# Seven block products for eight in groups 6 to 10 of the first feed-forward part, with that part's order written out, and block 2's first three groups moved to its end

## The chip, the cores and the metric

The kernel runs on one core of a Trainium2 chip. The metric is the device time of one execution in microseconds (us). A core has a matrix engine (PE, with its weight loads as PEld), a vector engine (DVE), an activation engine (ACT), a general engine (POOL) and an engine that issues most DMAs (SP). Each works through its own list of instructions in order and waits for the others by semaphores.

## The reference

One layer of a streaming encoder in fp32: 1024 prompt frames and 32 sample frames, model width 1024, feed-forward width 2816.

```python
x += 0.5 * gate1 * RMSNorm(SwiGLU_1(adaLN(RMSNorm(x))))    # first feed-forward part (FFN1)
x +=       gate2 * RMSNorm(W_out [mixerA ; mixerB](adaLN(RMSNorm(x))))
x += 0.5 * gate3 * RMSNorm(SwiGLU_2(adaLN(RMSNorm(x))))    # second feed-forward part (FFN2)
def swiglu(h, w_gate, w_up, w_down):
    return (jax.nn.silu(h @ w_gate) * (h @ w_up)) @ w_down
# shift, scale and gate of all three: SiLU(c) @ w_mod + b_mod   (1024 -> 9216)
```

Mixer A is a chunked attention of 8 heads, mixer B a sliding-window attention of 8 query and 2 key/value heads; one projection w_in (1024 -> 2304) feeds both. New key and value rows are outputs too.

## The kernel before

**Number format.** Every fp32 operand is split into a rounded part (hi, by ACT) and the rest (lo, by DVE), and a product is three matmuls: hi·hi, hi·lo, lo·hi (`mm3`, L339 to L341). So each weight tile that is loaded costs an ACT copy and a DVE subtraction before PE can use it, the "split".

**Tiling.** The 1056 frames are three token blocks: 0 and 1 of 384 columns, 2 of 288 (256 prompt and 32 sample). The 22 tiles of 128 feed-forward columns are 11 groups of two. For a group and a block the kernel forms gate and up (96 matmuls of the block's width), silu times up (`sl`, `gg`, DVE L904 and L907, ACT L903), and the down product (`dn`, 48 matmuls), which DVE adds into the block's accumulator `facc`.

**FFN1** (`ffn_plain`) goes through groups 0 to 7 with all blocks, then groups 8 to 10 with blocks 0 and 1, and last groups 8 to 10 with block 2, whose weights are loaded again. While block 2's groups run, block 0 and then block 1 get their residual, norm and next input (`between`: `resid` writes `f` by L485 and L488, `norm_h` writes `n` by L441 and `h` by L467, with a chain of small operations L348 to L352 for one over the root). The loads of w_in for the mixers are issued there too. Beside FFN1, generators that `step` moves on by one piece work out w_mod's product on DVE (`mod_aside`, L241 and L243), since no matmul is used for it.

**FFN2** (`ffn`) does groups 0 and 1 block by block, and groups 2 to 10 with all blocks as "fast" rounds. In those gate and up of blocks 0 and 1 are one product of two by two blocks (feed-forward tile, half of the model width, token block), made by seven block products instead of eight in a scheme of Strassen's kind: `STRASSEN` lists them, L595 issues their matmuls, `Mat` forms sums of weight blocks, `combos` the sums T1 to T4 of inputs. Block 2 has no partner and is done as usual with the same weight tiles (`g`, L595). The order of DVE, ACT and PE in the fast rounds is the order in which the code is written (`manual_schedule`); elsewhere a scheduler orders each engine's list when the kernel is built. In both, the list of an engine is fixed on the chip. The order of a round's stages is gate of the round, down of the one before, up of the round.

Of the kernel before, what the change touches and what calls it, by code (L numbers as in the profile page):

```python
# [78 lines left out]
def encoder_step(ctx: ExitStack, tc, x_prompt, x_sample, cache_a_k, cache_a_v, cache_b_k, cache_b_v,  # L79
# [109 lines left out]
    def mod_chunk(n):  # L189
        raws = []  # L190
        for g in range(2):
            r = t_tile("w", [128, 4, 512], "wm")
# [17 lines left out]
        coefs(n)  # L210

    def coefs(n):

        seg, half = divmod(n, 2)
        c0 = 8 * seg + 4 * half
        cs, ks = slice(c0, c0 + 4), slice(4 * half, 4 * half + 4)
        ve.tensor_tensor(modT[:, :, cs], modT[:, :, cs],
                         cst[:, None, cs].to_broadcast([128, 2, 4]), op=OP.add)
        sub, kind = divmod(seg, 3)
        if kind == 1:  # L220
            ve.scalar_tensor_tensor(acoef[:, sub, :, ks], modT[:, :, cs], 1.0,
                                    gain(2 * sub)[:, None, ks].to_broadcast([128, 2, 4]),
                                    op0=OP.add, op1=OP.mult)
        elif kind == 2:
            ve.scalar_tensor_tensor(gcoef[:, sub, :, ks], modT[:, :, cs], 1.0 if sub == 1 else 0.5,
                                    gain(2 * sub + 1)[:, None, ks].to_broadcast([128, 2, 4]),
                                    op0=OP.mult, op1=OP.mult)
# [1484 lines left out]
```

## Time and profile before

| | |
|---|---|
| median of 3 runs | 2184.54 us (2183.96 to 2186.63) |
| the profiled execution, its span | 2184.44 us, 2182.7 us |
| PE busy | 2123.9 us (97%) |
| DVE, ACT, POOL busy | 1403.6 (64%), 786.3, 171.8 us |
| TensorE clock granted, mean | 0.985 |

FFN1 takes the span from about 45 to 850 us, the mixers to about 1415, FFN2 the rest. Busy time is a share of an average over stages; a window of the trace tells which engine is full in one stage. A wait names the instruction that ended it.

### The profile page before, as it was taken

What the parts mean: (1) busy time and instruction counts of PE and PEld (TensorE: products, weight loads), DVE (VectorE), ACT (ScalarE), POOL (GpSimd) and SP (SyncE); (2) the same over time, 40 slices, a digit from 0 to 9 for tenths busy, and PEclk for the clock granted to TensorE, in tenths of its full rate; (3) what the DMA queues carried; (4) which work ended last, traced back from release to release, by engine and by line L of the source; (5) the groups of instructions that cost most, each with busy time, mean ns of one, the idle gap of its engine ahead of it and who ended that gap; (6) DMA issues with size and microseconds to landing.
All of it is one profiled execution on the core that took longest, in us unless ns stands there. A gap on an engine that the chain in (4) does not pass through costs nothing.

```text
span 2182.7 us, 34270 instructions
## 1 busy us (share of the span) xinstructions
PE 2123.9 (97%) x13796; PEld 2029.4 (93%) x13796; DVE 1403.6 (64%) x2783; ACT 786.3 (36%) x1654; POOL 171.8 (8%) x273
## 2 busy tenths in 40 slices
PE   6999999999999999899999899999999999999998
PEld 4999999999999999898888578999999999999997
DVE  5687667865343497677544776589666656566658
ACT  3411111111121254467544665365432222233225
POOL 1100000000000022100100323220000000000001
PEclk8999999999999999899999899999999999999999
DMA  9253334433121244100210202244311111111114
GB/s 319 103 155 116 107 97 135 136 91 115 55 78 58 87 152 141 60 25 26 69 31 26 84 22 86 98 160 129 113 62 55 39 59 39 58 59 39 39 59 140
DMA packets 178803, 192.35 MB, mean 88 GB/s; under 512 B 7788, under 2 KB 147476, under 8 KB 177492
## 3 DMA queue, kind: packets, MB, share of 16 engines
q1 hardware_dynamic: 178644, 190.16, 28.1%
q8 instruction: 108, 1.77, 0.3%
q14 instruction: 51, 0.42, 0.1%
HBM read 170.42 MB, written 22.86 MB: 89 GB/s over the span
## 4 chain that ended last, share of the span: by engine, by line
PE 88%; DVE 6%; DMA 3%; ACT 2%; issue 1%; POOL 0%; SPq 0%; DVEq 0%; ACTq 0%; POOLq 0%
PE g L595 5%; PE dn L339 4%; PE gate L341 4%; PE gate L340 4%; PE dn L340 4%; PE dn L341 4%; PE up L339 4%; PE up L341 4%; PE gate L339 4%; PE up L340 4%; PE ga L595 3%; PE gb L595 3%; PE gd L595 3%; PE dn L807 3%; PE dn L805 3%; PE dn L806 3%
## 5 line engine op out<-in xcount | busy, mean ns | idle before, releaser
L318 DVE TENSOR_TENSOR w<-raw,w 128x1024 fp32r<-128x1024 f32 x109 | 135.0, 1243 | 80.7 <-ACT w L317 80.6
L805 PE MATMUL dn<-gg,w 128*128 128x384 f32 (+1 forms) x528 | 170.1, 323 | 1.7 <-DVE facc L812 1.7
L339 PE MATMUL dn<-gg,w 128*128 128x384 f32 (+1 forms) x528 | 170.0, 324 | 1.0 <-DVE facc L934 0.9
L541 ACT ACTIVATE w<-raw 128x512 fp32r<-128x512 f32 x180 | 110.1, 626 | 169.0 <-issue 75.8
L806 PE MATMUL dn<-gg,w 128*128 128x384 f32 (+1 forms) x528 | 169.1, 321 | 1.8 <-DVE gg L700 1.8
L382 POOL TENSOR_TENSOR sq<-sq 128x384 f32<-128x384 f32 (+1 forms) x48 | 53.0, 1114 | 1491.2 <-ACT sq L378 1460.4
L340 PE MATMUL dn<-gg,w 128*128 128x384 f32 (+1 forms) x528 | 169.7, 321 | 0.6 <-DVE gg L907 0.6
L807 PE MATMUL dn<-gg,w 128*128 128x384 f32 (+1 forms) x528 | 168.9, 322 | 1.2 <-DVE w L542 1.2
L341 PE MATMUL dn<-gg,w 128*128 128x384 f32 (+1 forms) x528 | 169.4, 321 | 0.0
L317 ACT ACTIVATE w<-raw 128x1024 fp32r<-128x1024 f32 x109 | 114.4, 1056 | 145.1 <-PE up L341 48.8
L812 DVE TENSOR_TENSOR facc<-dn,facc 128x768 f32<-128x768 f32 (+1 forms) x120 | 106.5, 890 | 89.7 <-PE dn L807 89.7
L934 DVE TENSOR_TENSOR facc<-dn,facc 128x768 f32<-128x768 f32 (+1 forms) x120 | 106.0, 887 | 81.3 <-PE dn L341 81.3
L243 DVE SCALAR_TENSOR_TENSOR macc<-raw,csil,macc 128x512 f32<-128x512 f32 x196 | 137.7, 747 | 15.2 <-DMA raw<-in_w_mod_dram 14.8
L542 DVE TENSOR_TENSOR w<-raw,w 128x512 fp32r<-128x512 f32 x180 | 124.8, 705 | 19.5 <-ACT w L541 19.1
L903 ACT ACTIVATE sl<-gate 128x384 f32<-128x384 f32 (+1 forms) x66 | 30.5, 463 | 283.1 <-PE gate L341 280.3
L595 PE MATMUL g<-h_hi,w 128*128 128x288 f32 x576 | 123.2, 294 | 0.0
L340 PE MATMUL gate<-h,w 128*128 128x384 f32 x352 | 118.6, 337 | 1.9 <-DVE h L467 1.9
L339 PE MATMUL gate<-h,w 128*128 128x384 f32 x352 | 118.7, 337 | 0.0
L341 PE MATMUL gate<-h,w 128*128 128x384 f32 x352 | 118.3, 336 | 0.0
L339 PE MATMUL up<-h,w 128*128 128x384 f32 x352 | 118.1, 335 | 0.0
L341 PE MATMUL up<-h,w 128*128 128x384 f32 x352 | 118.1, 335 | 0.0
L340 PE MATMUL up<-h,w 128*128 128x384 f32 x352 | 117.9, 335 | 0.0
(318 smaller groups left out, 5787.5 us busy)
## 6 DMA issues: line engine op xcount, KB each, us to landing
raw<-in_w_gate_dram SPq DMA_DIRECT2D x58, 512.0 KB, 3.9
raw<-in_w_up_dram SPq DMA_DIRECT2D x58, 512.0 KB, 4.1
raw<-in_w_down_dram SPq DMA_DIRECT2D x58, 512.0 KB, 3.6
raw<-in_w_mod_dram SPq DMA_DIRECT2D x56, 512.0 KB, 3.9
raw<-in_w_in_dram SPq DMA_DIRECT2D x18, 512.0 KB, 4.4
wm<-in_w_mod_dram SPq DMA_DIRECT2D x8, 1024.0 KB, 7.1
raw<-in_w_out_dram SPq DMA_DIRECT2D x13, 512.0 KB, 4.6
xr<-xs SPq DMA_DIRECT2D x16, 384.0 KB, 3.5
```

The source lines that it names most:

```text
L243: ve.scalar_tensor_tensor(acc[j], r[:, kk], c, acc[j], op0=OP.mult, op1=OP.add)
L317: ae.activation(w[:, 0], r, AF.Copy)
L318: ve.tensor_sub(w[:, 1], r, w[:, 0])
L339: te.matmul(ps, w[:, 0, k], hi, start=start, stop=False)
L340: te.matmul(ps, w[:, 0, k], lo, start=False, stop=False)
L341: te.matmul(ps, w[:, 1, k], hi, start=False, stop=stop)
L541: ae.activation(w[:, 0], src, AF.Copy)
L542: deferred.append(lambda: ve.tensor_tensor(w[:, 1], src, w[:, 0], op=OP.subtract))
L595: te.matmul(ps, w[a][:, k, :], x[b][k], start=first and k == 0 and q == 0, stop=last and k == n - 1 and q == 2, skip_group_check=True)
L805: te.matmul(ps[:, s, :w], h[:, k % 4, :], g[:, 0, :w], start=q == 0, stop=False)
L806: te.matmul(ps[:, s, :w], h[:, k % 4, :], g[:, 1, :w], start=False, stop=False)
L807: te.matmul(ps[:, s, :w], l[:, k % 4, :], g[:, 0, :w], start=False, stop=q == 1)
```

## The change

FFN1 now uses `ffn` as well, under the key "h1". Its rounds are groups 0 to 2 with blocks 0 and 1, groups 3 to 10 with all three, and groups 0 to 2 with block 2 at the end (weights loaded again). Groups 6 to 10 are fast rounds. From the gate of group 3 to the gate of the first of block 2's rounds at the end, the order of DVE, ACT and PE is the written one; ahead of that and behind it the scheduler orders as before. The first round does gate and then up of a block, and up's weights lie in tiles `wu`. w_mod's product is made in pieces of 384 columns instead of 512, the first quarter of it by ACT; its last eight of 72 column tiles are worked out in FFN2. The hi and lo parts of inputs T1 to T3 are formed ahead of the first fast round and T4 in it. FFN1 has pools of its own (`FFN1`), and the mixers' pools are opened (`open_pools("mx")`) only behind it, ahead of the first loads of w_in. Splits are of 512 columns everywhere in FFN1 (before: 1024).

```diff
-STEPS = 6
+LAST = 3
+PLAIN = 6
+FFN1 = {"ux": 3, "r": 4, "w": 4, "g": 6, "s": 11}
...
-    open_pools("mx", **MIX)
+    open_pools("f1", **FFN1)
...
-    def rounds():
+    def rounds(key):
         both, n = (0, 1, 2), NF // 2
-        return [(g, (tb,)) for tb in both for g in range(LEAD)] + [(g, both) for g in range(LEAD, n)]
+        if key == "h3":
+            return [(g, (tb,)) for tb in both for g in range(LEAD)] + [(g, both) for g in range(LEAD, n)]
+        return [(g, (0, 1)) for g in range(LAST)] + [(g, both) for g in range(LAST, n)] + \
+            [(g, (2,)) for g in range(LAST)]
...
-        fast = {r for r, (g, t) in enumerate(plan) if len(t) == 3}
+        fast = {r for r, (g, t) in enumerate(plan) if len(t) == 3 and (key == "h3" or g >= PLAIN)}
+        fixed = (min(fast), len(plan) - 1) if key == "h3" else (LAST, NF // 2)
...
-            if (r, what) == (len(plan) - 1, "u"):
+            if (r, what) == (fixed[1], "u" if key == "h3" else "g"):
+                flush()
                 steady.close()
...
+            elif key == "h1" and r == 0:
+                mu = loaded[r, "u"]
+                mu.places = wide() + [t_tile("r", [128, 2, 4, 128], "w", F32R)]
+                for tb in blocks:
+                    need((key, tb))
+                    last = tb == blocks[-1]
+                    plain(r, "g", m, [tb], lambda k: None)
+                    plain(r, "u", mu, [tb], lambda k, last=last: last and ready(i + 2, k))
...
-    ffn1 = ffn_plain("h1", H1, F1, w1_gate, w1_up, w1_down, mod_rest, "h2", lambda tb: between(F1[tb], tb, 0, H2))
+    ffn1 = ffn("h1", H1, (("T3", "ux"), ("T1", "u"), ("T2", "ux"), ("T4", "u")), F1, lambda tb: u_tile(tb, "facc", F32),
+               w1_gate, w1_up, w1_down, "h2", lambda tb: between(F1[tb], tb, 0, H2, p1 if tb == 1 else pc), mod_rest)
...
+    open_pools("mx", **MIX)
     wkv, wq0, wv0 = split_vcols(w_in, 2048), load_qb(0), load_va(0)
```

Three places show how the lists move. The first is DVE at FFN1's start, where block 1's first norm is made (`rt`, `ry`: the small chain; `n`, `h`: block 1's input; `w`, `wu`: splits of weights). Before, from the last steps of the chain:

```order
L351 SCALAR_TENSOR_TENSOR rt<-rt,rv 128x3
L352 SCALAR_TENSOR_TENSOR ry<-rt,ry 128x3
L907 TENSOR_TENSOR gg<-sl,gg 128x384
L441 SCALAR_TENSOR_TENSOR n<-xt,acoef,pr 128x384 x8
L467 SCALAR_TENSOR_TENSOR h<-n,modT,h 128x384 x3
L932 COPY facc<-dn 128x768 x2
L467 SCALAR_TENSOR_TENSOR h<-n,modT,h 128x384 x3
```

And in the change:

```order
L384 SCALAR_TENSOR_TENSOR rt<-rt,rv 128x3
L385 SCALAR_TENSOR_TENSOR ry<-rt,ry 128x3
L475 SCALAR_TENSOR_TENSOR n<-xt,acoef,pr 128x384 x8
L501 SCALAR_TENSOR_TENSOR h<-n,modT,h 128x384
L576 TENSOR_TENSOR wu<-raw,wu 128x512 x3
L501 SCALAR_TENSOR_TENSOR h<-n,modT,h 128x384 x5
```

The lo parts of up's first three weight tiles now stand behind block 1's eight `n`. PE's list at the same place, in the change (`pss`, `pr`: sum and broadcast of block 1's norm):

```order
L404 MATMUL pss<-ones,sq 128x1 x6
L452 MATMUL pr<-ident,ry 128x128 x3
L632 MATMUL up<-h,wu 128x384 x4
L632 MATMUL gate<-h,w 128x384 x4
L632 MATMUL up<-h,wu 128x384 x32
L632 MATMUL up<-h,w 128x384 x12
L632 MATMUL gate<-h,w 128x384 x20
```

Block 1's `pr` stands behind 48 gate matmuls of block 0; before, it stood behind block 0's gate, up and the first of its down matmuls.

The second place is DVE at FFN1's end, in the second of block 2's three rounds (`dn` of 576 columns is block 2's). The change, from behind the add of the last down product of the first of those rounds to the lo parts of `gg` of the second, in two pieces that follow each other:

```order
L384 SCALAR_TENSOR_TENSOR rt<-rt,rv 128x3
L385 SCALAR_TENSOR_TENSOR ry<-rt,ry 128x3
L576 TENSOR_TENSOR wd<-raw,wd 128x512
L385 SCALAR_TENSOR_TENSOR ry<-rt,ry 128x3
L576 TENSOR_TENSOR wd<-raw,wd 128x512
L475 SCALAR_TENSOR_TENSOR n<-facc,acoef,pr 128x384 x8
L576 TENSOR_TENSOR wd<-raw,wd 128x512
L519 SCALAR_TENSOR_TENSOR facc<-facc,gcoef,pr 128x384 x6
L501 SCALAR_TENSOR_TENSOR h<-n,modT,h 128x384 x3
L519 SCALAR_TENSOR_TENSOR facc<-facc,gcoef,pr 128x384 x2
L501 SCALAR_TENSOR_TENSOR h<-n,modT,h 128x384 x2
L753 TENSOR_TENSOR sl<-sl,up 128x288
```

```order
L576 TENSOR_TENSOR w<-raw,w 128x512
L501 SCALAR_TENSOR_TENSOR h<-n,modT,h 128x384
L522 TENSOR_TENSOR facc<-facc,xr 128x768
L576 TENSOR_TENSOR w<-raw,w 128x512
L753 TENSOR_TENSOR sl<-sl,up 128x288
L576 TENSOR_TENSOR w<-raw,w 128x512 x2
L278 TENSOR_REDUCE modT<-pmt 128x3
L576 TENSOR_TENSOR wd<-raw,wd 128x512
L755 TENSOR_TENSOR gg<-sl,gg 128x288
L522 TENSOR_TENSOR facc<-facc,xr 128x768
L415 TENSOR_TENSOR sq<-sq 128x384
L755 TENSOR_TENSOR gg<-sl,gg 128x288
```

Before, block 0's `n` and `h` stood with block 2's adds, and block 1's residual (`facc<-facc,gcoef,pr`) in a later stretch:

```order
L934 TENSOR_TENSOR facc<-dn,facc 128x576 x2
L441 SCALAR_TENSOR_TENSOR n<-facc,acoef,pr 128x384 x8
L467 SCALAR_TENSOR_TENSOR h<-n,modT,h 128x384 x3
L934 TENSOR_TENSOR facc<-dn,facc 128x576
L467 SCALAR_TENSOR_TENSOR h<-n,modT,h 128x384 x2
L934 TENSOR_TENSOR facc<-dn,facc 128x576
```

So in the change the norm of block 0 and the residual of block 1 stand in one stretch ahead of one round's `gg`.

The third place is SP's list where FFN1 ends and the mixers' first loads stand. Before:

```order
L315 DMA raw<-in_w_down_dram 128x1024 x2
L482 DMA xr<-xs_123 128x768
L331 DMA raw<-in_w_in_dram 128x4x256
L482 DMA xr<-xs_123 128x768
L331 DMA raw<-in_w_in_dram 128x4x256
L482 DMA xr<-xs_123 128x768 x2
L315 DMA raw<-in_w_in_dram 128x8x128
```

The change:

```order
L618 DMA raw<-in_w_down_dram 128x1024 x2
L562 DMA xs_126<-facc 128x3072
L1401 DMA cbk<-in_cache_b_k_dram 128x128
L1402 DMA cbv<-in_cache_b_v_dram 128x128
L338 DMA bias_s<-skew_B 32x160 x8
L364 DMA raw<-in_w_in_dram 128x4x256 x2
L348 DMA raw<-in_w_in_dram 128x8x128
```

w_in's first loads moved behind block 1's write-back (`xs_126`), behind the caches and eight small bias loads; `cbk` waits for the last `gg` of FFN1 there, since the mixers' pools now take over FFN1's space.

More of the change, by code (lines that the diff above doesn't have):

```diff
@@ L209, in mod_chunk @@
                          axis=AX.X, op=OP.add)
[L210 to L227, printed above, removed]
@@ new lines, in encoder_step, with mod_all, fetch @@
+    depth = [2]
+    def mod_all(first, last):
+        pieces = [(c0, g) for c0 in range(first, last, 3) for g in range(4)]
+        tiles = {}
+        def fetch(i):
+            if i < len(pieces):
+                c0, g = pieces[i]
+                w = 128 * min(3, last - c0)
+                r = tiles[i] = h_tile([128, 2, 384], "wma")[:, :, :w]
+                dma.dma_start(r, w_mod[0, 256 * g:256 * (g + 1), 128 * c0:128 * c0 + w]
+                              .rearrange("(k p) n -> p k n", p=128))
+        fetch(0)
+        for i, (c0, g) in enumerate(pieces):
+            n = min(3, last - c0)
+            if g == 0:
+                acc = [s_tile([128, 384], "macc")[:, :128 * n] for _ in range(2)]
+            if i not in tiles:
+                fetch(i)
+                yield
+                yield
+            for j in range(i + 1, i + 1 + depth[0]):
+                if j not in tiles:
+                    fetch(j)
+            r = tiles.pop(i)
@@ L652, in encoder_step, with paces, ffn @@
+    def paces(key, r, what, blocks, n):
+        if r == 0 or len(blocks) == 1:
+            return 6 if key == "h3" else 5
+        if key == "h1" and r < PLAIN:
+            return 3 if what == "g" else 2
+        return int(what == "g" and (n not in (1, 4) or (key, r) == ("h1", PLAIN)))
     STRASSEN = [("A11", "B11", "a", 2), ("A12", "B21", "a", 2), ("S2", "T2", "b", 0), ("S1", "T1", "d", 0),
                 ("S3", "T3", "b", 0), ("A22", "T4", "e", 2), ("A21", None, None, 2), ("S4", "B22", "d", 0)]
-    def ffn(key, H, tags, F, facc, wg, wu, wd, key_out, after, beside):
-        plan = rounds()
+    def ffn(key, H, tags, F, facc, wg, wu, wd, key_out, after, behind):
+        plan = rounds(key)
@@ L672, in load @@
             if what == "d":
-                loaded[r, what] = Rows(wd, gi)
+                loaded[r, what] = Rows(wd, gi, key == "h1" and len(blocks) == 1)
             else:
@@ L1671, in finale, with behind @@
             yield
-    def beside():
-        for t in (1, 0, 2):
-            begin(("xp", t), tokens_first(t))
+    def behind(r, gi):
+        if r == 3 * LEAD:
+            begin("mod", mod_all(64, 72))
+        if gi == NF // 2 - 1:
+            for t in (1, 0, 2):
+                begin(("xp", t), tokens_first(t))
     open_pools("f2", **FFN2)
```

374 lines of the change are left out of this document (175 added, 199 removed).

## The prediction

> **What bounds the kernel now.** I read the page's first part and the chain of waits, then windows of FFN1 and FFN2, then PE's waits stage by stage.
>
> ```profile
> span 2182.7 us, 34270 instructions
> PE 2123.9 (97%) x13796; PEld 2029.4 (93%) x13796; DVE 1403.6 (64%) x2783; ACT 786.3 (36%) x1654; POOL 171.8 (8%) x273
> PE 88%; DVE 6%; DMA 3%; ACT 2%; issue 1%; POOL 0%; SPq 0%; DVEq 0%; ACTq 0%; POOLq 0%
> ```
>
> PE is busy all but 59 us and has 88% of the chain. The windows (length; then busy time of PE, PEld, DVE, ACT, POOL; granted clock, DMA share, GB/s) show which stage has room:
>
> ```profile
> 251.00:320.00 69.00, 69.00 (x439) 68.87 (x438) 47.19 (x74) 11.58 (x18) 0.00 (x0) 1.00 0.37 113
> 790.00:830.00 40.00, 38.30 (x286) 37.30 (x286) 36.19 (x66) 21.70 (x33) 6.52 (x5) 1.00 0.62 189
> 830.00:862.00 32.00, 32.00 (x253) 32.00 (x253) 26.66 (x50) 13.81 (x27) 10.63 (x9) 1.00 0.28 94
> 888.00:901.00 13.00, 9.25 (x40) 8.19 (x41) 10.78 (x38) 8.40 (x26) 3.39 (x7) 0.50 0.00 0
> 1641.00:1706.00 65.00, 65.00 (x411) 65.00 (x410) 39.54 (x63) 18.21 (x34) 0.00 (x0) 1.00 0.15 49
> ```
>
> The first row is a plain group of FFN1, the last a fast group of FFN2: PE is full in both, DVE is not. At FFN1's end (second and third row) DVE is nearly full too. At 888 to 901, after FFN1, PE runs at half clock. PE's waits from 734 to 930 us (waited for: us in total, times, longest), and the one of the start:
>
> ```profile
> PE gate L340 <- DVE h L467: 1.9, 1, 1.9
> ...
> PE pr L419 <- DVE ry L352: 2.4, 1, 2.4
> PE Sb L1166 <- ACT Ps L1241: 2.4, 1, 2.4
> PE pk L1410 <- DVE n L441: 1.9, 1, 1.9
> PE pv L1022 <- ACT h_hi L465: 1.1, 1, 1.1
> PE dn L339 <- DVE facc L934: 0.9, 2, 0.5
> PE dn L340 <- DVE gg L907: 0.6, 1, 0.6
> ```
>
> **The change, part by part.** *Fewer matmuls.* The lists hold 7088 matmuls of 128x384 before and 6968 after: 120 fewer (24 in each of five groups); those of 288 columns stay at 3648. The chain (start, us, what) gives the price of one, and the fast group's period:
>
> ```profile
> 1415.29 8.33 PE gate L595 x48
> 1604.82 3.19 PE g L595 x24
> ...
> 2058.69 3.19 PE g L595 x24
> ```
>
> 8.33/48 = 173.5 ns, so 120 x 0.1735 = **-20.8 us**. Check: from 1604.82 to 2058.69 there are seven fast periods of 64.84 us. A plain group of 144 matmuls of each width is 144 x (2 x 0.1735 + 3.19/24) = 69.1 us. The difference is 4.2 us, five times 21. The gain is there only where PE stays full.
>
> *Groups 3 to 10, in written order.* By counting the list with row durations DVE has 47 to 51 us of work in a fast group's 65 and 51 to 55 in a plain one's 69 (the trace has 47.2 in the row above), so its splits lie beside PE: 0. But mod's pieces stand in the same list, and a DVE that waits for one holds the splits behind it. The nearest row is all of DVE's waiting for w_mod before:
>
> ```profile
> L243 DVE SCALAR_TENSOR_TENSOR macc<-raw,csil,macc 128x512 f32<-128x512 f32 x196 | 137.7, 747 | 15.2 <-DMA raw<-in_w_mod_dram 14.8
> ```
>
> 14.8 us, all hidden there. I take 0, with ends -2 and +6 (four tenths uncovered). FFN2 gets mod's last eight column tiles of 72 and the deferred lo parts; DVE goes from 39.5 to at most 51 us of 65, so 0, from -3 to +3.
>
> *The start.* The first place in the document's lists: block 1's norm is due after 48 gate matmuls instead of after gate, up and some of down. Groups of DVE by shape (busy us, mean ns | idle before) in the window 44 to 110:
>
> ```profile
> L441 DVE SCALAR_TENSOR_TENSOR n<-xt,acoef,pr 128x384 f32<-128x384 f32 x8 | 4.3, 608 | 0.3 <-PE pr L419 0.3
> L467 DVE SCALAR_TENSOR_TENSOR h<-n,modT,h 128x384 fp32r<-128x384 f32 x6 | 4.6, 819 | 0.0
> L350 DVE TENSOR_TENSOR rt<-ry 128x3 f32<-128x3 f32 x6 | 1.0, 162 | 0.2
> ```
>
> PE stops at `pr` for the small chain, some 13 steps of 0.16 us = 2.1. Behind `pr` it has eight matmuls of `up` and `gate` (8 x 0.1735 = 1.4 us) until it needs the lo part of `wu`, which stands behind eight `n` (4.3), one `h` (4.6/6 = 0.8) and a split (0.7): 5.8, so 4.4 more. Then 32 of `up` cover the rest. Idle 6.5 instead of the 1.9 us above. What comes after such an idle is in the window:
>
> ```profile
> 75.40:78.60 3.20, 3.20 (x11) 3.20 (x11) 3.20 (x5) 0.91 (x3) 2.69 (x3) 0.52 0.03 5
> ```
>
> 3.2 us at 0.52 of the clock lose 1.5 us, before and after alike. So **+4.5** (+2 where the scheduler's early `n` finish sooner, +7 with a second half-clock stretch).
>
> [...]
>
> *FFN1's end.* The second place. All that stands there must be done by DVE between the last down product of block 2's first round and the lo parts of `gg` of its second, since the list is in order and begins behind that product's add. Durations from the groups of DVE in the window 734 to 905, and from the page for the split:
>
> ```profile
> L467 DVE SCALAR_TENSOR_TENSOR h<-n,modT,h 128x384 fp32r<-128x384 f32 x12 | 9.4, 835 | 0.0
> L485 DVE SCALAR_TENSOR_TENSOR facc<-facc,gcoef,pr 128x384 f32<-128x384 f32 x16 | 8.6, 607 | 0.0
> L441 DVE SCALAR_TENSOR_TENSOR n<-facc,acoef,pr 128x384 f32<-128x384 f32 x16 | 8.6, 605 | 2.4 <-PE pr L419 2.4
> L382 DVE TENSOR_TENSOR sq<-sq 128x384 f32<-128x384 f32 x8 | 7.1, 921 | 3.0 <-ACT sq L378 3.0
> L488 DVE TENSOR_TENSOR facc<-facc,xr 128x768 f32<-128x768 f32 x4 | 4.4, 1130 | 0.0
> L907 DVE TENSOR_TENSOR gg<-sl,gg 128x288 fp32r<-128x288 f32 x6 | 3.5, 590 | 0.0
> L904 DVE TENSOR_TENSOR sl<-sl,up 128x288 f32<-128x288 f32 x6 | 2.7, 446 | 0.6 <-PE up L341 0.5
> ...
> L542 DVE TENSOR_TENSOR w<-raw,w 128x512 fp32r<-128x512 f32 x180 | 124.8, 705 | 19.5 <-ACT w L541 19.1
> ```
>
> By busy time over count: 8 `n` and 8 `facc` of 0.54 = 8.6; 6 `h` of 0.78 = 4.7; 8 splits of 0.69 = 5.5; 2 `xr` adds of 1.1 = 2.2; 2 `sl` and 2 `gg` of 0.45 and 0.58 = 2.1; `sq` 0.9; a reduction and three small ones 1: 25.0 us. PE has meanwhile `pr` (0.7) and one up of 48 x 0.133 = 6.4; the next gate stands in its list behind the down product that waits. So PE idles some 17 us. The third round: DVE has `n`, `h`, four splits and two adds (14 us) against a gate and the first of up (9), and the first round is short by as little: +3 in all (0 to 7).
>
> Then the third place: w_in's loads stand behind `cbk`, which waits for the last `gg`, and behind eight bias loads. Landing times (KB each, us to landing, window 800 to 840):
>
> ```profile
> raw<-in_w_in_dram SPq DMA_DIRECT2D x7, 512.0 KB, 4.4
> bias_s<-skew_B SPq DMA_DIRECT2D x6, 20.0 KB, 3.2
> ```
>
> 3.2 + 4.4 + a split of about 2 (ACT, then DVE) = 9.6, of which the last down products cover 48 x 0.133 = 6.4 at most, less where the pool is freed late: 5 idle (2 to 8). Two idles of this length cost about 1.5 us of half clock each, with some overlap 2 in all. The end after: 17 + 3 + 5 + 2 = 27 (20 to 36). Before: the waits above 9.3 us less the 2.4 of `Sb` inside the mixers, 6.9; the half clock at 888 to 901 (9.25 busy x 0.5 = 4.6): 11.5. Those go, since w_in's products with blocks 0 and 1 then cover block 2's norm. So **+15.5** (+8 to +24).
>
> *Sum* against the profiled execution, 2184.44 (its span and 1.7 around it; the median 2184.54 is the same): -20.8 + 4.5 + 15.5 + 0 = -0.8, **2183.6 us**.
>
> **Rivals.** *The gain arrives (27%).* If DVE's burst costs little (operations run faster while PE is idle, PE's windows above are full almost wherever DVE has 36 of 40), the end costs no more than before: -20.8 + 4.5 + 1 = -15, **2169**, from 2162 to 2177. For it: before, the same norms at 790 to 862 cost 1.7 us of PE. Against it: there they stood over two more rounds of block 2's work, as the lists show.
>
> *FFN1's end decides, and it is slower (22%).* DVE's burst ahead of the second `gg` plus w_in's loads behind it. At the upper ends, 36 - 11.5 = 24.5, with +4.5 and -20.8: +8, **2192**, up to 2199. It decides from the point where idle and half clock between the last add of group 10 and the first w_in product exceed 28 us (20.8 - 4.5 + 11.5).
>
> *The written order stalls on mod (6%).* DVE waits for w_mod's pieces in groups 3 to 10 and PE for splits: +6 on the sum, **2189**. The first rows would be waits of PE for `w` in FFN1, where there is none before from 110 to 734. Against: SP's loads stand a stage ahead.
>
> *The counts are other than said:* excluded, 120 fewer.
>
> **Numbers.** The forecast has 45%, with its own range 2177 to 2190. Less than 0.2% (4.4 us) can't be told from no change. Of the 45, 12 lie below 2180.1, 25 inside and 8 above 2188.9. With the first rival's 27 faster, 39% faster; with 2 of the second and 1 of the third inside, 28% the same; the rest, 33%, slower. Range 2166 to 2197: it takes most of both rivals and leaves a tenth at each side.
>
> **What would show it.** *Matmuls:* gate and up of 384 columns in groups 6 to 10 as `ga`, `gb`, `gd`, `ge`; periods of 64.8 us there, 69.1 in groups 3 to 5. *Start:* waits of PE for `ry` or `wu` of some 6.5 us before 70. *End:* one wait of PE for `gg` or `sl` between 8 and 18 us long, DVE full in that window; then one of 2 to 8 us for w_in; no idle at block 2's norm. *Middle:* no wait of PE from 110 to its group 10. I am wrong if that single wait is under 8 us, or if PE waits in the middle for more than 6.

## The result, and the profile after

| | before | with the change |
|---|---|---|
| median | 2185.11 us (2183.96 to 2186.63, 4 runs) | **2214.04 us** (2202.26 to 2216.47, 4 runs) |
| ratio, with its 95% interval | | **1.0121** (1.0085 to 1.0158) |
| profiled span | 2182.7 us | 2212.6 us |

The change makes the kernel 1.2% slower; the prediction said 2183.6 us, and 2197 at the most. Two executions far outside all others (8430.64 us of e12 below, 11736.45 of the kernel before beside e16 and e17) stand outside the ratios. The page of the changed kernel: its span, the busy time of each engine, and the shares of the chain of waits.

```profile
span 2212.6 us, 34628 instructions
PE 2121.8 (96%) x13676; PEld 2023.1 (91%) x13676; DVE 1503.8 (68%) x3077; ACT 860.8 (39%) x1846; POOL 173.0 (8%) x273
PE 84%; DVE 10%; DMA 2%; ACT 2%; issue 1%; SPq 1%; POOL 0%; DVEq 0%; ACTq 0%; POOLq 0%
```

PE has the 120 fewer matmuls (13796 to 13676), yet its busy time fell by 2.1 us and not by 20.8, and it is idle for 2212.6 - 2121.8 = 90.8 us where it was idle for 58.8. DVE rose from 6% to 10% of the chain. Busy time that falls by less than the work taken out means that the rest of the work ran slower: mostly the clock, as the next rows show.

Windows of the two kernels by stage show where (length; busy time of PE, PEld, DVE, ACT, POOL; granted clock, DMA share, GB/s). The rows are FFN1's start from its first gate to 130 us, its middle, its last 130 us up to its last down product, and the 100 us behind that. After:

```profile
42.50:130.00 87.50, 75.10 (x418) 72.87 (x417) 65.04 (x175) 41.33 (x84) 13.43 (x14) 0.86 0.59 195
130.00:741.40 611.40, 606.58 (x3768) 604.29 (x3767) 418.55 (x703) 165.46 (x308) 0.00 (x0) 1.00 0.27 82
741.40:871.40 130.00, 106.95 (x689) 102.90 (x687) 110.88 (x213) 53.57 (x95) 29.24 (x23) 0.88 0.36 116
871.40:971.40 100.00, 94.83 (x692) 91.06 (x692) 56.20 (x169) 45.61 (x122) 10.29 (x18) 0.93 0.27 85
```

The same stages before:

```profile
44.70:130.00 85.30, 83.39 (x521) 82.19 (x520) 64.44 (x131) 36.57 (x71) 13.21 (x14) 0.98 0.42 140
130.00:720.40 590.40, 590.40 (x3691) 589.41 (x3690) 354.28 (x550) 100.69 (x154) 0.00 (x0) 1.00 0.34 102
720.40:850.40 130.00, 128.30 (x882) 127.30 (x882) 95.44 (x160) 49.80 (x71) 24.91 (x18) 1.00 0.45 142
850.40:950.40 100.00, 92.11 (x660) 87.01 (x659) 63.84 (x188) 51.79 (x146) 16.03 (x23) 0.90 0.15 46
```

Length less PE's busy time is the idle time of a stage: 12.4 us at the start (1.9 before), 4.8 in the middle (0), 23.1 at the end (1.7), 5.2 behind it (7.9). The granted clock tells the second loss. PE's busy time inside the stretches at half clock, of which half is counted as lost (an estimate: in the trace before, matmuls of 384 columns start every 0.32 us from 75.2 to 78.1 us, at half clock, and every 0.17 behind it), sums over the trace's clock records to 13.8 us at the start (3.4 before), 3.4 in the middle (0), 20.5 at the end (0), 12.9 behind it (15.3). In the whole span it is 84.9 us against 52.9. So the account of the +29.9 us of span is: products -20.8, idle +32.0, half clock (84.9 - 52.9)/2 = +16.0; sum +27.2. 2.7 us are in none of the three.

PE's waits, from FFN1's start to 130 us, and then from 760 to 920 us (waited for: us in total, times, longest):

```profile
PE dn L874 <- ACT facc L879: 6.9, 1, 6.9
PE pr L452 <- DVE ry L385: 2.9, 1, 2.9
PE up L632 <- ACT wu L575: 2.0, 1, 2.0
PE gate L632 <- DVE h L501: 0.7, 1, 0.7
```

```profile
PE pmt L277 <- DVE modT L278: 7.3, 1, 7.3
PE dn L874 <- ACT gg L754: 5.6, 2, 5.4
PE up L632 <- DVE w L576: 3.8, 3, 2.7
PE gate L632 <- DVE sl L753: 1.8, 1, 1.8
PE pss L404 <- DVE sq L417: 1.7, 1, 1.7
PE pr L452 <- DVE ry L385: 1.6, 2, 1.0
PE dn L875 <- DVE gg L755: 1.2, 1, 1.2
PE pv L1024 <- ACT w L366: 0.6, 1, 0.6
...
```

**The largest stall** is the second of block 2's rounds, as forecast. DVE's timeline there (start us, us, what, and the idle time ahead of it in brackets):

```profile
811.60 0.69 DVE L576 TENSOR_TENSOR wd<-raw,wd 128x512 fp32r<-128x512 f32 x1 [0.72 <-ACT wd L575]
...
812.88 4.28 DVE L475 SCALAR_TENSOR_TENSOR n<-facc,acoef,pr 128x384 f32<-128x384 f32 x8
...
817.69 3.23 DVE L519 SCALAR_TENSOR_TENSOR facc<-facc,gcoef,pr 128x384 f32<-128x384 f32 x6
...
833.05 0.55 DVE L278 TENSOR_REDUCE modT<-pmt 128x3 f32<-128x384 f32 x1
...
836.96 0.45 DVE L755 TENSOR_TENSOR gg<-sl,gg 128x288 fp32r<-128x288 f32 x1
```

DVE works without a pause from 811.6 to 837.4, through block 0's `n`, block 1's residual, and only then the reduction `modT` and the `gg` that PE's down products need. PE waits for 5.37 us (for `gg` by way of ACT), 7.30 (for `modT`, which frees the buffer of PE's transposes `pmt`) and 1.20: 13.9 us, with two down matmuls and three transpositions between them. Windows of 3.41 us of the same place, laid so that the records' changes of the clock (to half at 823.8, back at 847.7) fall on their borders:

```profile
820.45:823.86 3.41, 0.00 (x0) 0.00 (x0) 3.41 (x7) 1.26 (x3) 1.57 (x1) 0.99 0.21 39
827.28:830.69 3.41, 0.00 (x0) 0.00 (x0) 3.41 (x4) 0.45 (x1) 2.06 (x1) 0.50 0.01 5
837.52:840.93 3.41, 3.41 (x17) 3.41 (x16) 2.82 (x8) 1.15 (x2) 0.00 (x0) 0.50 1.05 437
844.34:847.75 3.41, 3.41 (x16) 3.41 (x15) 2.07 (x10) 0.00 (x0) 0.00 (x0) 0.51 0.00 0
847.75:851.17 3.42, 3.42 (x29) 3.42 (x28) 2.27 (x4) 1.50 (x3) 0.00 (x0) 1.00 0.00 0
```

PE works again from 835.75 on, but three full windows, to 847.75, pass at half clock (16 or 17 matmuls of a window instead of 29). The stall's own time is 13.9 us; the half clock, counted as above, takes half of the 13.7 us that PE was busy between 823.8 and 847.7, another 6.8.

**The stall that was not forecast** is at 115 us. ACT's timeline:

```profile
111.47 1.11 ACT L267 ACTIVATE macc<-wma,csil 128x384 f32<-128x384 f32 x2
120.00 1.12 ACT L267 ACTIVATE macc<-wma,csil 128x384 f32<-128x384 f32 x2 [7.42 <-DMA wma<-in_w_mod_dram]
121.03 1.49 ACT L879 ACTIVATE facc<-dn 128x768 f32<-128x768 f32 x2
```

In the change ACT makes the first of the eight steps of each piece of w_mod's product (`macc`: 38 operations on ACT and 266 on DVE, so an eighth of them and not the quarter that the description of the change names), and ACT's list has a `macc` ahead of the copies of the first down products into `facc`. That `macc` waits 7.42 us for its piece of w_mod; the copies stand behind it, and PE's next `dn` waits 6.86 us for them. Half clock begins inside this wait, at 117.2, and lasts to 127.4.

### The profile page after: what moved, and what is told of

It reads as the page before. It is cut to its first block, busy times and chain, and to the rows that moved or that the text cites. A ratio compares the mean times of both kernels' runs of the same rounds, so it can differ in the third digit from the quotient of the medians.

```text
span 2212.6 us, 34628 instructions
## 1 busy us (share of the span) xinstructions
PE 2121.8 (96%) x13676; PEld 2023.1 (91%) x13676; DVE 1503.8 (68%) x3077; ACT 860.8 (39%) x1846; POOL 173.0 (8%) x273
## 4 chain that ended last, share of the span: by engine, by line
PE 84%; DVE 10%; DMA 2%; ACT 2%; issue 1%; SPq 1%; POOL 0%; DVEq 0%; ACTq 0%; POOLq 0%
PE g L632 8%; PE up L632 7%; PE dn L874 7%; PE dn L876 7%; PE dn L875 7%; PE gate L632 6%; PE gb L632 5%; PE ga L632 5%; PE gd L632 5%; PE po L1068 3%; PE ge L632 3%; PE pq L372 2%; PE S L1107 2%; PE pq L374 2%; PE pq L373 2%; DVE w L576 2%
## 5 line engine op out<-in xcount | busy, mean ns | idle before, releaser
L874 PEld LDWEIGHTS dn<-gg,w 128*128 128x128 f32 x1008 | 190.0, 189 | 12.3 <-ACT facc L879 7.5
L876 PEld LDWEIGHTS dn<-gg,w 128*128 128x128 f32 x1008 | 189.9, 189 | 1.7 <-DVE w L576 1.7
L875 PEld LDWEIGHTS dn<-gg,w 128*128 128x128 f32 x1008 | 190.1, 189 | 0.7 <-DVE gg L755 0.7
L269 DVE SCALAR_TENSOR_TENSOR macc<-wma,csil,macc 128x384 f32<-128x384 f32 (+1 forms) x266 | 148.5, 609 | 11.3 <-ACT macc L267 10.2
L632 PEld LDWEIGHTS g<-h_hi,w 128*128 128x128 f32 x896 | 148.1, 188 | 0.0
L632 PE MATMUL gate<-h,w 128*128 128x384 f32 x768 | 139.5, 337 | 0.7 <-DVE h L501 0.7
L632 PEld LDWEIGHTS gate<-h,w 128*128 128x128 f32 x768 | 133.0, 188 | 1.3 <-DVE h L501 1.2
L632 PE MATMUL g<-h_lo,w 128*128 128x288 f32 x448 | 131.9, 294 | 0.0
L632 PE MATMUL gb<-t,w 128*128 128x384 f32 x672 | 127.5, 338 | 2.2 <-DVE sl L810 2.2
L632 PE MATMUL ga<-h,w 128*128 128x384 f32 x672 | 126.5, 335 | 0.0
L632 PE MATMUL up<-h,w 128*128 128x384 f32 x696 | 126.3, 335 | 0.0
L632 PEld LDWEIGHTS up<-h,w 128*128 128x128 f32 x696 | 120.4, 188 | 0.4 <-DVE w L576 0.2
```

Of the source, the lines that this page charges most:

```text
L269: ve.scalar_tensor_tensor(acc[j], r[:, kk], c, acc[j], op0=OP.mult, op1=OP.add)
L632: te.matmul(ps, w[a][:, k, :], x[b][k], start=first and k == 0 and q == 0, stop=last and k == n - 1 and q == 2, skip_group_check=True)
L874: te.matmul(ps[:, s, :w], h[:, k % 4, :], g[:, 0, :w], start=q == 0, stop=False)
L875: te.matmul(ps[:, s, :w], h[:, k % 4, :], g[:, 1, :w], start=False, stop=False)
L876: te.matmul(ps[:, s, :w], l[:, k % 4, :], g[:, 0, :w], start=False, stop=q == 1)
```

## Experiments

All runs below are against the kernel before, whose median was 2183.5 to 2184.4 us in them. "The change" is the kernel with the diff above, 2214.0 us; its own runs lie between 2202.3 and 2216.5, so a median a few microseconds below it shows little by itself, and where the runs of the two overlap (e2, e3, e5, e9) the reading rests on the traces. `paces` is the function that says how many pieces of side work (norms, residuals, w_mod, loads) the code moves on beside each product.

**The first four separate the products, the start, the end and the clock.**

*e1: the change without its products.* Groups 6 to 10 are plain again; order, pools and pieces stay.

```diff
-fast = {r for r, (g, t) in enumerate(plan) if len(t) == 3 and (key == "h3" or g >= PLAIN)}
+fast = {r for r, (g, t) in enumerate(plan) if len(t) == 3 and key == "h3"}
```

(The code that forms T1 to T4 in FFN1 goes with it.)

> FFN1 keeps the changed order, pools and rounds, but groups 6 to 10 are made with the usual eight products (no sums of inputs or weights there). Theory (the products give their 20.8 us, and the time is lost at FFN1's start and end): 20.8 us longer than the change, about 2235 us (2228 to 2240), idle of PE at the start and at the end as in the change. Rival (the products' gain is eaten inside groups 6 to 10): within 6 us of the change's 2214.

Measured: 2228.09 us, ratio 1.0204 (1.0152 to 1.0255), span 2229.7. The last 130 us of its FFN1:

```profile
757.50:887.50 130.00, 108.00 (x691) 104.92 (x689) 98.59 (x187) 52.14 (x91) 29.20 (x23) 0.87 0.38 124
```

22.0 us of idle at the end and the clock at 0.87: the same loss as with the products, so it has nothing to do with them. Between the two spans lie 17.1 us, between the medians 14.1; e1 has only two runs, 6.7 us apart. Most of what is missing from 20.8 stands in FFN1's middle, where the change has 1.7 us more of idle time than e1 (4.8 and 3.1) and a half-clock stretch of 3.4 us (1.7 lost) that e1 has not. It begins at the first fast group, where PE waits 2.17 us for `sl` (`gb`, L810). So the products bring about what was worked out, to within the few microseconds by which runs differ.

*e2: w_mod's work begun one round later*, so that ACT's `macc` is not ahead of the first `facc`.

```diff
         if r == 0:
             in_order.close()
+        if r == 1:
             begin("mod", mod_and_bias())
```

> w_mod's product beside FFN1 begins one round later, so that its first pieces no longer stand ahead of the first copies of facc on ACT. Theory: the 6.86 us that PE waits for ACT's facc copy at 115 us go, with the 10.2 us of half clock that follow (5.1 lost): 12 us less than the change, about 2202. Rival (w_mod's late loads stop another instruction instead): under 4 us less, with a new wait of PE of 5 us or more in groups 0 to 3.

Measured: 2205.47 us, 1.0102 (1.0063 to 1.014), 8.6 us better than the change. Its start:

```profile
42.20:130.00 87.80, 82.28 (x470) 80.36 (x468) 49.65 (x143) 41.25 (x81) 13.41 (x14) 0.92 0.44 150
```

Idle 5.5 instead of 12.4 us, and no wait for ACT's `facc`: the cause of the stall at 115 us is shown. But w_mod's rest comes later too: a wait for `modT` of 8.7 us (7.3 in the change) stands in FFN1's end, where the idle time rises from 23.1 to 26.5, and two more of 2.5 and 2.0 behind it.

*e3: four of block 2's rounds at the end instead of three* (`LAST = 4`), so that the norms meet a further round.

```diff
-LAST = 3
+LAST = 4
```

> Groups 0 to 3 (not 0 to 2) go without block 2 and are made up for at FFN1's end: 20 us more of PE's work beside the two norms there, and some 13 us more of DVE's. Theory (DVE has too much to do beside the last rounds): idle of PE from 130 us before FFN1's end falls from 23 by 6 to 12 and half clock with it, 8 to 15 us less than the change, about 2203. Rival (the order, not the amount, makes the stall: DVE's list has both norms in one stretch wherever it stands): idle stays over 18, time within 5 of 2214.

Measured: 2204.68 us, 1.0096 (1.0059 to 1.0133), 9.4 us better. Idle at the end 17.8 us, busy at half clock 10.8 (23.1 and 20.5 in the change). One more round takes a part of the burst and not the whole.

*e4: five measured stalls of PE* in plain groups 3 to 5, where PE is full: a transposition, then 1, 3, 5, 8 and 12 operations of DVE on its result (with one more behind them), and a second transposition that needs the last.

```diff
+    STALLS = {(3, "u"): 1, (4, "g"): 3, (4, "u"): 5, (5, "g"): 8, (5, "u"): 12}
...
+            if key == "h1" and (r, what) in STALLS:
+                flush()
+                stall(STALLS[r, what])
```

> Five stalls of PE are put into the plain groups 3 to 5 of the change, where PE has none: a transpose, a chain of 1, 3, 5, 8 and 12 small DVE operations on it, and a transpose that waits for the chain. They add work and leave none out. Theory (any idle of about 2 us in a busy stretch costs a stretch of half clock): stalls of 2 us and more are each followed by 3.4 us or more at half clock, shorter ones by none. [...]

Measured, in one profile (2229.09 us, its stalls included). PE's timeline shows three of the five stalls; the others are 2.20 and 4.36 us:

```profile
276.11 0.48 PE L721 MATMUL pmt<-ident,sl 128*128 128x128 f32 x1 [2.31 <-DVE sl L719]
...
327.12 0.33 PE L721 MATMUL pmt<-ident,sl 128*128 128x128 f32 x1 [2.27 <-DVE sl L719]
...
410.81 0.48 PE L721 MATMUL pmt<-ident,sl 128*128 128x128 f32 x1 [5.64 <-DVE sl L719]
```

The stalls of 2.31 and of 2.27 us are equal, and one is followed by half clock (its matmul takes 0.48 us) and the other is not. Windows of 3.41 us, laid as before by the times at which the clock in the records changes, show how the two differ; each pair is the window with the stall and the one after it (at 350.58 and 354.00 the two windows of the stall of 4.36 us):

```profile
272.08:275.49 3.41, 1.06 (x8) 0.63 (x6) 2.07 (x6) 1.69 (x4) 0.00 (x0) 1.00 0.00 0
275.49:278.90 3.41, 2.79 (x9) 2.80 (x10) 1.12 (x3) 0.80 (x2) 0.00 (x0) 0.50 0.26 75
323.28:326.69 3.41, 1.57 (x13) 1.30 (x11) 2.16 (x7) 2.77 (x5) 0.00 (x0) 1.00 0.00 0
326.69:330.10 3.41, 2.98 (x18) 2.98 (x19) 0.94 (x3) 0.00 (x0) 0.00 (x0) 1.00 0.35 113
350.58:354.00 3.42, 1.53 (x12) 1.27 (x10) 1.42 (x5) 0.96 (x2) 0.00 (x0) 1.00 0.00 0
354.00:357.41 3.41, 0.94 (x6) 0.94 (x7) 3.17 (x10) 0.00 (x0) 0.00 (x0) 1.00 0.01 2
405.20:408.61 3.41, 0.00 (x0) 0.00 (x0) 3.21 (x11) 0.65 (x2) 0.00 (x0) 1.00 0.00 0
408.61:412.02 3.41, 1.21 (x4) 1.21 (x5) 3.21 (x10) 0.00 (x0) 0.00 (x0) 0.50 0.00 0
```

Where PE was busy for 1.06 us of a window, the next ran at half clock; with 1.57 us it did not. The stall of 4.36 us gives both: its first window had 1.53 us of work and the clock stayed, its second 0.94, and the next (357.41 to 360.82) ran at half clock. So in this trace the length of a stall alone does not tell what follows it. Nor does the work of one window: in the trace before, the window 71.69 to 75.10 had 1.53 us too, and half clock followed (0.51 from 75.10 to 78.52).

In the change PE was busy for 3.37 of the 3.41 us of the window ahead of the start's half clock; 1.50 of them are twelve sums of one column (`pss`). The granted clock was 1.00 in it and 0.50 in the next (55.79 to 59.21):

```profile
52.38:55.79 3.41, 3.37 (x31) 3.04 (x29) 3.04 (x6) 1.86 (x6) 1.20 (x1) 1.00 0.47 192
```

What these sums have to do with it is not shown. Near the end of the change's FFN1 one figure of work has both outcomes: 1.62 us in the window 782.83 to 786.24, and full clock stayed; 1.62 us from 789.66 to 793.07, and half clock followed.

**Single edits for the start and the end.**

*e5: `wu`'s splits begun with block 0's gate*, ahead of block 1's norm in DVE's list.

```diff
-plain(r, "g", m, [tb], lambda k: None)
+plain(r, "g", m, [tb], lambda k: mu.begin(("A11", "A12")[k]))
```

> The change with one edit: the splits of up's first weight tiles (wu) are begun in the first round's gate, so that they no longer stand behind block 1's norm, and PE's list has 46 of block 0's 48 up matmuls ahead of block 1's pr. Theory (the start loses to the norm of block 1 coming too early in the lists): the idle of 2.88 and 1.96 us at 56 to 62 us falls below 2 in all and the half clock of 13.65 us behind it to 6.8 or less: 4 to 7 us less than the change. Rival (block 1's norm is late wherever it stands, since only 16.7 us of block 0's matmuls cover it): 4 to 6 us of idle move to block 1's gate, time within 3 us of the change.

Measured: 2212.44 us, 1.0131 (1.0111 to 1.0151), no difference from the change that could be told. The waits at block 1's first norm go from 2.88 + 1.96 + 0.67 = 5.5 us to 1.04 + 1.44 + 2.77 = 5.3: the same work of DVE, and PE now waits for block 1's `h` instead of `wu`, as the rival said. ACT's wait at 115 us is shorter (2.4 instead of 6.9 us).

*e6: the end in written order too, with a slower pace* of the side work there.

```diff
-            if (r, what) == (fixed[1], "u" if key == "h3" else "g"):
+            if (r, what) == (fixed[1], "u"):
...
-        fixed = (min(fast), len(plan) - 1) if key == "h3" else (LAST, NF // 2)
+        fixed = (min(fast), len(plan) - 1) if key == "h3" else (LAST, len(plan) - 1)
...
-            return 6 if key == "h3" else 5
+            return 6 if key == "h3" else 5 if r == 0 else 2
```

> The change with one edit at FFN1's end: the written order holds up to the last round (there the scheduler took over at block 2's rounds), and the norms go on by two pieces per product. Amount of work as in the change. Theory (the order of DVE's list makes the stall): the idle of 13.9 us at 820 to 836 falls below 4, idle in the last 130 us of FFN1 from 23.1 to 6 to 10, half clock from 20.5 to under 7: 18 to 24 us less, about 2193. Rival (DVE has too much work there, in whatever order): idle stays over 15, time 2205 or more.

Measured: 2227.68 us, 1.0201 (1.0171 to 1.0231), worse than the change. Its last 130 us:

```profile
746.70:876.70 130.00, 107.53 (x639) 103.11 (x637) 90.96 (x175) 45.48 (x79) 23.58 (x18) 0.84 0.35 118
```

Idle is 22.5 us, about as in the change (23.1), in many waits of 2 to 4 us (`pr`, `gg`, `pss`) instead of one long one, and busy time at half clock rises to 35.1. PE's small norm matmuls (`pss`, `pr`) now stand where they are written, and PE waits there for the chain; in the change the scheduler places them. Spread over short stalls, about the same idle time (22.5 and 23.1 us) came with more half clock here, 35.1 us against 20.5.

*e7 and e8: w_mod later, `wu` early and the written end together; e8 also with `LAST = 4`.*

> Three edits together: w_mod one round later, wu early, FFN1's end in written order. Theory (three separate losses, each with its half clock): the gains add up, about 9 + 5 + 21 = 35 less than the change, 2179 (2172 to 2188). Rival (a late DVE moves on to the next wait): under two thirds of the sum, 2190 or more.

> As the three edits together, and groups 0 to 3 without block 2 at first, made up for at FFN1's end. Theory (with the order mended the norms are covered): within 4 us of the three edits alone. Rival (DVE is still short of time beside block 2's rounds): 4 us or more faster than the three edits alone.

Measured: 2235.47 us, 1.0232 (1.0217 to 1.0247), and 2234.53, 1.0237 (1.0219 to 1.0254). To e6's loss comes in e7 that w_mod's rest slides behind FFN1: DVE still works on `macc` at 906 us, at 923 us PE waits 9.2 us for `sq` on POOL in the mixers, and from 921 to 948 it runs at half clock. e8 has no such stretch, but 28.9 us of idle time in its last 130 us of FFN1 (23.1 in e7).

*e9: PE filled instead of stalled.* 100 matmuls (13.3 us at 0.133) go ahead of the down product of the second of block 2's rounds; the real products overwrite what they leave.

```diff
+            if key == "h1" and r == NF // 2 + 1 and mp == 0:
+                hi = H[2][0]
+                for i in range(FILL):
+                    te.matmul(ps[:, 0, :w], m.w[1, 0][0][:, i % 4, :], hi[i % KT], start=True, stop=True, skip_group_check=True)
```

> The change with work added: 100 matmuls of 288 columns (13.3 us) whose result is overwritten, in PE's list where it waits for DVE's burst, ahead of the down products of block 2's second round. DVE's work is the same, so the wait ends when it did. Theory (PE's clock falls because it has too little to do, and the half clock costs as much as the idle there): the 23.9 us of half clock behind the wait go, 7 to 10 us less than the change although PE does more. Rival (the clock goes by something else, or the time up to FFN1's end is DVE's anyway): within 3 us of the change, or longer.

Measured: 2206.48 us, 1.0100 (1.0085 to 1.0116): **7.6 us faster than the change by the medians, although PE has 13.3 us more to do.** The runs of the two overlap, so the trace has to show it:

```profile
733.90:863.90 130.00, 119.11 (x822) 115.74 (x820) 114.81 (x220) 56.16 (x99) 29.51 (x23) 0.97 0.40 127
```

The filling takes the place of the wait (idle 10.9 instead of 23.1), and the busy time at half clock falls from 20.5 to 6.4 us. 13.3 - 12.2 - 14.1/2 = -6.0 us by these rows; the spans differ by -6.8. So the clock behind the stall is a loss of its own, shown apart from the stall.

*e10: only the pace.* The scheduler orders the end as in the change, but the code moves on two pieces of side work per product there instead of five.

```diff
-            return 6 if key == "h3" else 5
+            return 6 if key == "h3" else 5 if r == 0 else 2
```

> The change with one number: in block 2's rounds at FFN1's end the norms go on by two pieces per product instead of five; the scheduler still orders the end. DVE's list then has block 1's residual behind the second round's gg and block 1's n and h behind FFN1's last add. Theory (what stands ahead of one gg makes the stall): the wait at 820 to 836 falls from 13.9 to about 5; the norm of block 1 comes later but is covered by w_in's products with block 0, and the time is 8 to 15 us less than the change. Rival (what is put off is missed later, as in the written end): idle behind FFN1's end grows by as much, time 2210 or more.

Measured: **2193.49 us, 1.0046 (1.0031 to 1.0061): 20.5 us from one number.** The last 130 us:

```profile
714.50:844.50 130.00, 122.26 (x834) 120.37 (x833) 111.19 (x215) 52.84 (x93) 22.96 (x18) 0.97 0.40 129
```

Idle 7.7 us, 6.8 at half clock. DVE's work in the window is the same as in the change (111 us); only its order against block 2's rounds differs. That shows the cause of the loss at the end: not the norms, and not block 2's place at the end, but that five pieces at a time push them all in front of one `gg`. A part moves on: behind FFN1 PE is idle for 10.9 us (5.2 in the change). With that, and half of the busy time at half clock (6.8 and 7.7 us), the end and the 100 us behind it cost 25.9 us, against 45.0 in the change and 17.2 before. Three waits are left: 2.7 us for `w`, 3.6 for `gg`, and 6.1 (3.35 + 0.62 + 2.08) for w_in and block 1's norm. e6 has the same pace and differs from this run by the written order alone; it is 34 us slower, so the pace pays in the scheduler's order only.

**Combinations, to see whether a version beats the kernel before.**

*e11: w_mod later, `wu` early, pace 2, and w_mod's pieces faster in the first rounds* (4 and 3 per product to round 4, instead of 3 and 2). *e12: the same with pace 3.*

> The scheduler's end with two pieces per product, wu early, w_mod one round later and on by one piece more per product in groups 0 to 4. Theory (separate losses): about 9 + 4 + the gain of two pieces per product alone less than the change, 2185 to 2195. Rival: w_mod's product, begun later, reaches into FFN1's end and the mixers and costs what the late start won.

> As the run before it with three pieces per product at FFN1's end: there block 1's residual stands in one stretch with block 0's h, behind the first gg of the second round. Theory (the stretch ahead of a gg decides): 2 to 6 us longer than with two pieces per product. Rival (what is put off past FFN1's end costs more): shorter than with two.

Measured: e11 2189.39 us (2186.14 to 2196.78, 10 runs), **1.0026 (1.0016 to 1.0036), with e17 below the best of all**, and still slower than before; e12 2210.75 (the middle of three runs), 1.0113 (1.0088 to 1.0137). e11 from FFN1's first gate to 130 us, and its last 130 us:

```profile
42.50:130.00 87.50, 81.65 (x482) 80.31 (x481) 57.30 (x159) 44.36 (x86) 13.48 (x14) 0.96 0.51 162
711.60:841.60 130.00, 121.27 (x829) 119.44 (x828) 110.82 (x215) 53.03 (x93) 22.95 (x18) 0.97 0.40 132
```

e12 at its end:

```profile
738.60:868.60 130.00, 107.72 (x682) 104.26 (x681) 107.09 (x209) 54.09 (x94) 32.89 (x23) 0.87 0.38 120
```

Between pace 2 and 3 lies as much idle time again: 22.3 us against 8.7. It is not the one stall of the change: the longest wait is 7.0 us for `sq`, since PE's list has block 1's sum (`pss`) ahead of the last round's up products there and behind them in e11; 4.0 and 3.6 us are for `gg`. The pace is no dial with a smooth optimum; one step moves a piece of a norm across a product. In e11 idle time is 77.2 us against 58.8 before, and the half clock is back where it was (52.0 against 52.9), so the products' 20.8 and the idle time's 18.4 nearly cancel. By this the span should be 2.9 us below the kernel before; it is 1.7 above. 4.6 us are in neither, and this stays open.

*e13: `wu`, pace 2, and filling matmuls (25 at the stall, 27 ahead of w_in's first product). e14: `wu`, pace 2, `LAST = 4`. e15: e13 with w_mod later.*

> wu early and two pieces per product at FFN1's end, and work added whose result is overwritten: 25 matmuls (3.3 us) ahead of the down products of block 2's second round, 27 of 256 columns (3.2 us) ahead of the mixers' first product with w_in. w_mod begins as in the change. Theory (what is left beside the products' 20.8 us is idle of 2 to 4 us at four places, each with its half clock; two of them keep the clock now): the 4 us of wu early come off the 2193.5 of two pieces per product alone, and 2 to 4 more from the clock: 2184 to 2188. Rival (the filling itself delays what waits behind it): 2190 or more.

> wu early, two pieces per product at FFN1's end, groups 0 to 3 without block 2 at first; nothing added. Block 1's n and h stand ahead of FFN1's last add then, not behind it. Theory (amount and order both count): idle behind FFN1's last down product falls from 10 to about 5, and 3 to 8 us come off: 2182 to 2187. Rival (with two pieces per product there is nothing left to win by a fourth group; its splits and a later w_mod cost): 2190 or more.

> As the first of this call, with w_mod begun one round later (no faster pace afterwards). Theory: 2 to 5 us less than that one, 2180 to 2185, since the wait for ACT's first facc copies goes. Rival: w_mod's pieces that are left at FFN1's end cost DVE as much there.

Measured: 2196.49 us, 1.0054 (1.0039 to 1.0069); 2201.54, 1.0071 (1.005 to 1.0092); 2204.28, 1.0092 (1.0075 to 1.0109). None beats e10's 2193.5. Filling bought nothing where the stall is short: e13 has less idle time than e10 in its span (72.0 and 79.5 us), but more busy time at half clock (69.3 and 58.1). With a fourth round PE's `pmt` waits for w_mod's `macc` (3.8 us in two) and its down products for `gg` (3.8 and 3.2). No run has `wu` and pace 2 alone, so what each further edit costs by itself is not shown. In e15, which differs from e13 by w_mod alone, w_mod's rest falls into the mixers, as in e7:

```profile
892.00:918.00 26.00, 11.28 (x53) 9.86 (x52) 19.91 (x64) 10.80 (x30) 8.28 (x12) 0.54 0.11 46
```

PE works 11.3 of 26 us there, at 0.54 of the clock. This half clock began at 894.1 us. PE was full for one window of 3.41 us before the clock was back at 1.00, where in the change it was full for three:

```profile
914.58:917.99 3.41, 3.41 (x18) 3.15 (x18) 3.35 (x11) 2.96 (x10) 2.16 (x6) 0.50 0.00 0
917.99:921.41 3.42, 3.42 (x31) 3.42 (x31) 2.38 (x10) 0.39 (x1) 0.61 (x2) 1.00 0.00 0
```

*e16: `wu`, pace 2, and w_mod's pieces faster still (5 and 4 per product in the first three rounds, 4 and 3 after). e17: the same with group 5 fast as well (`PLAIN = 5`).*

> wu early, two pieces per product at FFN1's end, and w_mod's product on faster in groups 0 to 5 (five and four pieces per product in groups 0 to 2, four and three in 3 to 5), so that it is done before the first fast rounds instead of at FFN1's end and beyond; it begins as in the change. Nothing added or left out. Theory (w_mod's rest beside the last rounds and the mixers' first products takes DVE's time there): idle behind FFN1's last down product from 10 to about 5, no wait for w_mod's transposes there; 4 to 8 us less than the 2189.4 of the best so far: 2181 to 2186. Rival (w_mod's loads and DVE's 62 us of work in a plain group of 69 stop PE in groups 0 to 5): 2190 or more, with 6 us or more of new idle from 130 to 330 us.

> As the run before it, with group 5 made by seven products as well. Theory: another 24 matmuls of 173.5 ns less, 4.2 us, less some 1 us for the sums' own waits: 2 to 4 us below it. Rival (w_mod then reaches to group 9 and DVE's sums collide with it): within 1 us of it, or longer.

Measured: 2201.86 us, 1.0079 (1.0064 to 1.0094), and 2189.99 (2185.32 to 2195.58, 10 runs), 1.0027 (1.0018 to 1.0037). With w_mod done early idle time stands in the middle, 6.6 us from 130 to 330 us and 6.0 from there to the end's beginning; 5.1 of it are waits for w_mod's pieces. A sixth fast group saves 24 products, 4.2 us; e17 is 11.9 faster than e16. By the two traces idle time (83.8 to 81.0) and half clock (66.4 to 58.7, half of it) are 6.7 us of the rest; why they fall is not shown. e11 and e17 can't be told apart. No version ran faster than the kernel before.

## Why the prediction was wrong

**Fewer matmuls, -20.8: right.** The counts are as said (120 fewer of 384 columns), and e1 finds 17.1 us between the spans, with 3.4 of the rest in idle time and half clock of the middle. The period of a fast group in FFN1 is 65.2 to 65.7 us and not 64.8, since six of w_mod's transpositions (`pmt`, 1.0 us in a group) stand in it; those stood in the plain groups before.

**Middle, 0: too good.** PE waits 4.8 us and loses 1.7 to the clock, +6.5 in all, a little beyond the end of +6. DVE's splits were covered, as said. 2.2 us of the wait are for `sl` of the first fast group, where DVE's part of the scheme begins, which is in no term; 2.6 are for w_mod's pieces (`modT` 2.0, `macc` 0.6), which the prediction had taken as hidden. FFN2, 0: 750.7 us against 748.6 from its first gate to its last down product, inside the ±3.

**The start, +4.5: the mechanism right, the sum short by 9.** Idle time rose from 1.9 to 12.4 us and the loss to the clock from 1.7 to 6.9; less the 2.2 us by which the first gate is earlier, that is +13.5. The idle time at block 1's norm was to be 6.5 us and is 5.5, in the places named (`ry`, then `wu`, then `h`). Two things failed. The half clock was put at 3.2 us as before; it lasted 13.7 us. It set in at 55.8 us, as the first stall began, behind the window (52.38 to 55.79) with block 1's one-column sums; with the three stalls in them the next windows had 0.58, 1.45 and 2.71 us of work, all at 0.50 of the clock. And the wait of 6.86 us at 115 us is in no term, nor the 10.2 us at half clock around it. The prediction asked what waits behind a w_mod piece on DVE and priced that as a rival, at 6% and in groups 3 to 10. The same question for ACT, to which the change gives an eighth of w_mod's work, was not asked. In e2 that wait is gone.

**FFN1's end, +15.5: the mechanism right, the size short by 12.** DVE's burst was worked out at 25.0 us and took 25.8 (811.6 to the end of the last `gg` at 837.4); the idle time was to be 17 us and the three waits and two for `pr` make 15.5; the wait for w_in was to be 5 us and is 0.6 (`pv`), with 1.7 for a norm's sum (`pss`) ahead of it. The step that failed is the line "two idles of this length cost about 1.5 us of half clock each, with some overlap 2 in all". It took the price of a 1.9 us stall, one stretch of 3.2 us, for a stall of 14. In its place stand 20.5 us busy at half clock in the end and 12.9 behind it: 16.7 us lost where 2 were forecast. Against that the half clock before was 15.3 in that stretch, not the 9.25 counted. With idle 23.1 + 5.2 and 16.7 the stage costs 45.0, before 17.2: **+27.8**.

Over the whole kernel the prediction's terms had idle time rise by 22.7 us and the loss to half clock fall by 2.6 (2 at the end, for the 4.6 before); the runs have +32.0 and +16.0. So 18.6 of the 30 us by which the time was missed are the price of half clock, 9.3 idle time.

**The rivals.** "FFN1's end decides, and it is slower" (22%) is the one that happened, and past its own point of decision: between the last add of group 10 and the first w_in product (786.4 to 875.4) there are 22.1 us of idle and 10.3 of half clock, beyond its 28. Its price of 2192 was the idle time at its upper bound with almost no half clock. "The gain arrives" (27%) fell, and its reasons with it: DVE's operations ran no faster in the burst (eight `n` took 4.28 us, as before), and that the same norms stood over more rounds before, which the prediction had named as the evidence against it, fits e10, where spreading them gives most of the loss back. "The written order stalls on mod" (6%): in its place, groups 3 to 10, the waits for w_mod are the 2.6 us above; the long one came in another place and on another engine. Its test for the end, one wait of 8 to 18 us, failed by its letter: the longest is 7.3 us, since the burst shows as waits of 5.4, 7.3 and 1.2. The other test, no wait of PE from 110 us to its group 10, found the 6.9 us at 115 us, and rightly so: that is where a term was missing. With the 4.8 us of the middle these are more than the 6 that it gave as a sign of being wrong, and 7.3 is under its 8.

**On half clock.** The prediction went by one row of the trace before: 1.9 us of idle, and behind them 3.2 us at 0.52 of the clock. That was a true reading, and e4 bears it out (a stall of 2.31 us was followed by half clock, with 1.06 us of work in its window). What that row could not tell is how long half clock lasts around a longer stall. The change's trace has stretches of 3.4, 6.8, 10.2, 13.7 and 23.9 us, each a whole multiple of 3.41, and the longest belongs to the stall of 13.9 us. For how long PE is full before the clock returns is open: three windows of 3.41 us here (the rows at 837 to 848), one in e15.

## What to carry to other kernels

Read a list in order from the place of each wait: whatever stands ahead of the one instruction that PE needs, and isn't done when PE gets there, is PE's idle time, on every engine that was given work (here ACT too, with a DMA behind it). Price a stall as its idle time plus half of PE's busy time at half clock around it in the trace, 6.8 us for the stall of 13.9 here, and look for such stalls first: the pace of the side work, one number, was worth 20.5 us, as much as all of the products saved. A saving on a full engine arrives (17 of 20.8 us did, by one pair of traces), but it pays only for what its new order costs.

## What the runs showed of the hardware that was not expected

- In the traces before and with the change every stretch at half clock inside FFN1 lasts a whole multiple of 3.41 us: 3.4 before, and 3.4, 6.8, 13.7, 10.2 and 23.9 with the change. In e4 a stall of 2.31 us was followed by half clock and one of 2.27 was not; their windows had 1.06 and 1.57 us of work. In the change a window with 3.37 us of busy time, 1.50 of it sums of one column, was followed by half clock. Runs of the changed kernel scatter from 2202 to 2216 us; why is not shown.
- Half clock was seen while PE was full: 0.50 for three windows at 837 to 848 us, and for one in e15 (914.58 to 917.99). 13.3 us of matmuls whose result nobody uses shortened the profiled span by 6.8 us (e9).
- Open: 2.7 us of the change's loss and 4.6 us of e11's are neither in PE's idle time, nor in the clock's records, nor in the counts. e1, without the products, has 3.3 us of the same kind, so they do not come from the products.
